# Hybrid gMLP/SSD block: dt moved into the exponent of the decays, x copied by ScalarE, products inside the chunk issued two steps at a time, ScalarE's decays listed by pairs

## The chip, the cores and the metric

The kernel runs on one core of a Trainium2 chip. The metric is the device time of one execution in microseconds (us), the median of three runs. A profile records one further execution: its rows give start and duration of the instructions of TensorE (PE, with its weight loads as PEld), VectorE (DVE), ScalarE (ACT), GpSimd (POOL) and of the DMA queues.

## What is computed

One layer of a decoder trunk over 1024 positions of width 1024 in float32: an input projection, a chunked gMLP branch, a Mamba-2 (SSD) branch, their gated merge and an output projection. The change touches the SSD branch alone. It has 32 heads of 64 channels in 8 groups of 4 heads, and walks the sequence in 8 chunks of 128 positions:

```python
xd = x * dt[..., None]
a_cs = cumsum(dt * a)                      # inside a chunk
cb = einsum('clgn,csgn->cgls', cc, bc)     # C_l . B_s
y_diag = einsum('cgls,cgrls,csgrp->clgrp', cb, exp(a_cs[l] - a_cs[s]) for s <= l, xd)
chunk_states = einsum('csgn,cgrs,csgrp->cgrpn', bc, exp(a_cs[-1] - a_cs[s]), xd)
state = state * exp(a_cs[-1]) + chunk_states      # over the chunks
y_off = einsum('clgn,cgrpn,cgrl->clgrp', cc, prev_states, exp(a_cs))
y = y_diag + y_off + x * d_skip
```

## The kernel before

**Stages.** Up to about 905 us of the span the kernel forms the input projections. Then comes the SSD stage, and behind it the projection of the SSD branch, the merge and the output. In the SSD stage TensorE alternates between the SSD work and the projection of the gMLP branch (`proj_a`), which is drawn from a generator: one `draw` issues two matmuls of 512 columns into the two banks `pma`. There are 192 draws; they fill TensorE's list between pieces of SSD work.

**Steps.** The SSD work is cut into 32 steps, `order[n] = (g, s)`: group g and a pair s of chunks. The order takes two groups side by side, (0,0), (1,0), (0,1), (1,1), ..., so s runs from 0 to 3 within eight steps, and steps 2k and 2k+1 are the same pair of chunks of two groups. A step consists of:

- `fetch`: loads `dcy`, the cumulative sums of 4 heads by 256 positions broadcast to 128 partitions, and `sl`, the slices of B, C, x and z. Five sets of buffers go round.
- `mask` (lines L1155 and L1159): two ACT instructions write `ea` = exp(a_cs) from `dcy`; then one POOL select overwrites the upper triangle of `dcy` with -1e30, in place, so it can't begin before both have read it.
- `decay` (L1167): eight ACT instructions turn `dcy` into exp(dcy - a_cs[s]), in place, so they can't begin before the select is done.
- `prep`: TensorE forms C.B in bank `pc`, and transposes B into `pc` and x into bank `px`; DVE multiplies `dcy` by C.B (L1183), and forms x·dt (`xd`) and x·dt·exp(..) (`xe`) from `px` (both L1186); ACT copies the transposed B into `bn` (L1190). Accesses to one bank keep their order in the program, so `bn` waits for L1183.
- `front`: sixteen matmuls of 64 columns `yi` <- `xd`, `dcy` (the product inside the chunk), then what strips are due (`pq`, matmuls of 32 columns that sum squares for a later norm), then `sp` <- `bn`, `xe` (the chunk states); DVE adds `sp` to the state (`add_state`, L1236), forms `y` from `yi` (L1216), and POOL scales the state for the next addition (`mul_state`, L1228).
- `back`: TensorE multiplies the states by C into `yn`; DVE forms `ym` = `yn`·`ea` (L1262); POOL adds it to `y` (L1264) and multiplies by the gate into `yz` (L1265). For every odd s the squares of `yz` (ACT, L1289) and their sum (POOL, L1293) follow some steps later, and once a group a root on POOL (L1320).

**What sets the order.** TensorE's instructions stand in program order. `link(key, f)` ties each instruction of ACT (`"A"`), DVE (`"V"`) and POOL (`"G"`) in these steps behind the one linked before it on that engine: the order in which the code names them is the order in which the engine's list holds them. An instruction that waits therefore holds up all linked ones behind it.

The loop of step n goes: `front(n)`; then `ahead_of(n)`, which lists the decays of step n+2, the first `mul_state` of step n+1, a sum or a root if one is due, and the mask of step n+3; then 4 or 5 draws; `back(n)`; `prep(n+2)`; `fetch`. So between the select of one step and that of the next POOL's list holds one whole step of other work.

**Banks.** Of PSUM's eight banks six rotate under the tag `bk` and two under `px`; `bank()` sends every fourth request to `px`.

Of the kernel before, what the change touches and what calls it, by code (L numbers as in the profile page):

```python
# [8 lines left out]
F32 = mybir.dt.float32  # L9
# [26 lines left out]
def hybrid_kernel(  # L36
# [493 lines left out]
    def bank(name):  # L530

        if pairs_done:
            pairs_done.append(name)
            if len(pairs_done) % 4 == 2:
                return psum.tile([P, 512], F32, name=name, tag="px", bufs=2)
        return psum.tile([P, 512], F32, name=name, tag="bk", bufs=6)

# [3 lines left out]
    def later(delay, f, *a):  # L541
        tasks.append((slot[0] + delay, f, a))
# [172 lines left out]
    def dt_part2(dth, adt):  # L715
        n = NCH * NH
        pa = bank("pacs")
        mm(pa[:, 0:n], tri, adt)
        mm(pa[:, n : 2 * n], ones, adt)
        V.tensor_scalar_mul(nacs, pa[:, 0:n], -1.0)  # L720
        A.activation(cd, pa[:, n : 2 * n], AF.Exp)
        V.tensor_add(dde, pa[:, n : 2 * n], nacs)
        A.activation(dde, dde, AF.Exp)
        V.tensor_mul(dde, dde, dthq)
        later(3, dt_part3)

    def dt_part3():
# [401 lines left out]
    class Group:  # L1129


        def __init__(self, g):
            self.g, self.pre, self.st, self.yz, self.y = g, {}, None, {}, {}

        def fetch(self, s):
            g, nm = self.g, f"{self.g}_{s}"
# [24 lines left out]

        def decay(self, s):

            dcy, sub = self.pre[s][1], fac(nacs, self.g, s)
            for i in range(2):
                for h in range(HPG):
                    link("A", lambda: A.activation(dcy[:, h, i, :], dcy[:, h, i, :], AF.Exp,  # L1167
                                                   bias=sub[:, i, h : h + 1]))

        def prep(self, s):  # L1170
            g, nm = self.g, f"{self.g}_{s}"
            sl, dcy, ea = self.pre[s]
            px, pc = bank(f"px{nm}"), bank(f"pc{nm}")
            for i in range(2):
                tsl = slice(i * P, (i + 1) * P)
                mm(pc[:, i * P : (i + 1) * P], sl[:, 1, tsl], sl[:, 0, tsl])
                tp(pc[:, 256 + i * P : 256 + (i + 1) * P], sl[:, 1, tsl], ident)
                tp(px[:, i * 256 : i * 256 + P], sl[:, 2, tsl], ident)
                tp(px[:, i * 256 + P : i * 256 + 256], sl[:, 3, tsl], ident)
            x4 = px.rearrange("p (i h w) -> p i h w", i=2, h=HPG)  # L1180
            xs = []
            d3 = dcy.rearrange("p h i l -> p h (i l)")
            link("V", lambda: V.tensor_tensor(d3, d3, pc[:, 0:256].unsqueeze(1).to_broadcast([P, HPG, 256]), op=ALU.mult))  # L1183
            for v, f in (("xd", dthq), ("xe", dde)):
                t = p2x.tile([P, 512], F32, name=f"{v}{nm}", tag=v, bufs=3)
                link("V", lambda: V.tensor_tensor(t.rearrange("p (i h w) -> p i h w", i=2, h=HPG), x4,  # L1186
                                    fac(f, g, s).unsqueeze(3).to_broadcast([P, 2, HPG, HD]), op=ALU.mult))
                xs.append(t)
            bn = p2x.tile([P, 256], F32, name=f"bn{nm}", tag="bn", bufs=3)
            link("A", lambda: A.copy(bn, pc[:, 256:512]))  # L1190
            self.pre[s] = (sl, dcy, bn, xs[0], xs[1], ea)

        def front(self, s):

            g, nm = self.g, f"{self.g}_{s}"
            sl, dcy, bn, xd, xe, ea = self.pre[s]
            yi = bank(f"yi{nm}")
# [356 lines left out]
    def draw(n):  # L1554
        for _ in range(n):
            left[0] -= next(fill, 1) is None
# [6 lines left out]
    def ahead_of(n):  # L1563

        with tc.high_priority():
            decays(n + 3)
            if n + 1 < len(order) and order[n + 1][1]:
                groups[order[n + 1][0]].mul_state(order[n + 1][1], 0)
            for _ in range(1 if n < 29 else 2):
                beside_step()  # L1570
            masks(n + 4)

    def step(n, *fs):
        for f in fs:
            item(getattr(groups[order[n][0]], f), order[n][1])

    draw(6)
    for n in range(2):
        step(n, "front")
        ahead_of(n)  # L1580
        draw(10)
    for n in range(len(order)):
        if n > 1:
            step(n, "front")
            ahead_of(n)
            draw(6 if n == 2 else 4 + n % 2)
# [5 lines left out]
        fetch(n + 6)  # L1592
    while tasks or work or posts:
        draw(2)
        run_tasks()
        beside_step()
        while posts:
            p, q, sq = posts.pop(0)
            p.post2(q, sq)


    room.extend(ea_r[0] + [st_tag])
# [470 lines left out]
```

## Time and profile before

| | |
|---|---|
| median of three runs | 1361.64 us (1361.04 to 1362.76) |
| profiled execution, its own time | 1362.27 us |
| its span, first to last instruction | 1360.4 us |
| granted TensorE clock, mean | 0.998 |
| first and last product inside the chunk (`yi`) | at 910.8 and 1106.8 us |

The span is what the trace covers; the 1.9 us beside it lie outside the first and the last instruction. Rows of the timeline give start, duration, engine, line and tiles; `x8` is the number of instructions merged into a row; what stands in brackets is the idle time before and what ended it. A matmul's recorded duration is longer than its share of TensorE, because matmuls overlap in the pipeline: what a matmul costs is read from the distance of two starts. In a row that groups instructions the number behind `|` is their busy time and then the mean duration of one in ns, and behind the second `|` stands the idle time in front of them with what ended it.

### The profile page before, as it was taken

The page shows a single profiled execution, that of the slowest core. Times are in us where ns is not written, and L with a number is a line of the kernel's source. Part 1 is how long each engine was busy: PE and PEld are TensorE (multiplying, and loading weights), DVE is VectorE, ACT ScalarE, POOL GpSimd, SP SyncE. Part 2 cuts the span into 40 slices and gives each one's busy share as a digit, 9 for nine tenths or more (in the row PEclk, how much of TensorE's full clock was granted, in tenths as well). Part 3 has the DMA queues.
Part 4 walks back from the last instruction along what each step waited for, and adds up shares of the span by engine and source line. Part 5 has one row for each costly group of instructions (what it writes and reads, how often), then busy time and mean ns, then how long its engine had stood idle before and what let it go on. Part 6 is the DMA issues. An engine that isn't in the chain of part 4 may idle for free.

```text
span 1360.4 us, 20108 instructions
## 1 busy us (share of the span) xinstructions
PE 1347.0 (99%) x6907; PEld 1114.4 (82%) x6907; DVE 1056.1 (78%) x1731; ACT 800.4 (59%) x1446; POOL 196.1 (14%) x193
## 2 busy tenths in 40 slices
PE   8999999999999999999999999999999999999997
PEld 6688888888888888888888888888888888888886
DVE  4776786787777898688887788358888877959976
ACT  5754666666657665466576655486877834233453
POOL 1000000000000000000000000007798981000002
PEclk9999999999999999999999999999999999999999
DMA  9675444333345667777656866489889878888913
GB/s 292 177 248 142 134 124 124 117 119 122 101 132 155 193 184 231 248 216 246 202 192 193 244 204 186 154 289 318 302 297 311 306 256 291 313 261 317 381 45 124
DMA packets 249577, 288.64 MB, mean 212 GB/s; under 512 B 16860, under 2 KB 196484, under 8 KB 249476
## 3 DMA queue, kind: packets, MB, share of 16 engines
q1 hardware_dynamic: 174868, 203.80, 47.0%
q10 hardware_dynamic: 74544, 83.57, 18.0%
q8 instruction: 54, 0.88, 0.3%
q14 instruction: 47, 0.39, 0.1%
q0 software_dynamic: 64, 0.00, 0.0%
HBM read 199.82 MB, written 87.49 MB: 211 GB/s over the span
## 4 chain that ended last, share of the span: by engine, by line
PE 93%; POOL 3%; DMA 1%; issue 1%; ACT 1%; DVE 1%; SPq 0%; POOLq 0%; DVEq 0%; ACTq 0%
PE xcb L585 6%; PE xz L585 6%; PE xuz L585 6%; PE xx L585 6%; PE xg L585 6%; PE pma L82 5%; PE ox L1914 3%; PE yuz L585 3%; PE yx L585 3%; PE ycb L585 3%; PE yp L1722 3%; PE yz L585 3%; PE vx L990 3%; PE yg L585 3%; PE oy L1914 2%; PE x0p L1722 2%
## 5 line engine op out<-in xcount | busy, mean ns | idle before, releaser
L1159 POOL TENSOR_SCALAR_AFFINE_SELECT dcy<-dcy 128x1024 f32<-128x1024 f32 x32 | 35.3, 1103 | 788.7 <-ACT ea L1155 788.7
L1167 ACT ACTIVATE dcy<-dcy,nacs 128x128 f32<-128x128 f32 x256 | 78.3, 389 | 2.9 <-POOL dcy L1159 2.4
L1183 DVE TENSOR_TENSOR dcy<-dcy,pc 128x1024 f32<-128x1024 f32 x32 | 39.0, 1218 | 8.0 <-PE pc L85 5.8
L1265 POOL TENSOR_TENSOR yz<-y,sl 128x512 f32<-128x512 f32 x32 | 44.7, 1396 | 2.5
L82 PE MATMUL pma<-yh,wah 128*128 128x512 f32 x128 | 43.2, 418 | 0.0
L82 PE MATMUL pma<-yh,wal 128*128 128x512 f32 x128 | 42.6, 413 | 0.0
L82 PE MATMUL pma<-yl,wah 128*128 128x512 f32 x128 | 40.2, 395 | 0.0
L1155 ACT ACTIVATE ea<-dcy 64x512 f32<-64x512 f32 x64 | 39.8, 622 | 0.4
L1190 ACT COPY bn<-pc 128x256 f32<-128x256 f32 x32 | 11.9, 371 | 46.4 <-DVE dcy L1183 44.9
L1060 ACT ACTIVATE ac<-ac 128x1024 f32<-128x1024 f32 x32 | 33.9, 1060 | 8.1 <-DVE ac L1058 7.9
L1264 POOL TENSOR_TENSOR y<-y,ym 128x512 f32<-128x512 f32 (+1 forms) x32 | 37.4, 1170 | 1.8 <-DVE ym L1262 1.8
L1058 DVE SCALAR_TENSOR_TENSOR ac<-c2x,cwt,ac 128x1023 f32<-128x1023 f32 (+2 forms) x24 | 30.7, 1278 | 8.8 <-ACT ac L1056 8.7
L1058 DVE SCALAR_TENSOR_TENSOR ac<-c2cb,cwt,ac 128x1023 f32<-128x1023 f32 (+2 forms) x24 | 30.7, 1278 | 8.2 <-ACT ac L1056 8.0
L1929 POOL TENSOR_TENSOR r<-r,fnw 128x512 f32<-128x512 f32 x4 | 6.1, 1534 | 207.3 <-ACT junk L1927 207.3
L82 PE MATMUL yi<-dcy,xd 128*64 128x128 f32 x512 | 35.0, 279 | 0.0
L1262 DVE TENSOR_TENSOR ym<-yn,ea 128x512 f32<-128x512 f32 (+1 forms) x32 | 19.9, 621 | 18.2 <-PE yn L82 18.0
L1653 DVE SCALAR_TENSOR_TENSOR yn<-yn,par,rb 128x512 f32<-128x512 f32 x32 | 26.1, 822 | 9.1 <-DMA yn<-yb_d 9.1
L82 PE MATMUL sp<-xe,bn 128*128 128x256 f32 x112 | 32.7, 409 | 0.0
L82 PEld LDWEIGHTS yn<-sl,st 128*128 128x128 f32 x224 | 29.8, 191 | 2.8 <-POOL st L1228 0.4
L82 PEld LDWEIGHTS yi<-dcy,xd 128*64 128x64 f32 x512 | 27.3, 136 | 5.7 <-issue 3.2
L1058 DVE SCALAR_TENSOR_TENSOR ac<-c1cb,cwt,ac 128x1023 f32<-128x1023 f32 (+2 forms) x24 | 30.6, 1276 | 1.3 <-ACT ac L1056 1.3
L1022 ACT ACTIVATE vm<-vm,vr 128x128 f32<-128x128 f32 x64 | 25.5, 483 | 10.1 <-DMA vm<-v_d 9.6
(2983 smaller groups left out, 4368.4 us busy)
## 6 DMA issues: line engine op xcount, KB each, us to landing
sl<-s_d SPq DMA_DIRECT2D x32, 768.0 KB
s_d<-ac ACTq DMA_DIRECT2D x32, 512.0 KB
wb_d<-wbb ACTq DMA_DIRECT2D x32, 512.0 KB
dcy<-acs_d SPq DMA_DIRECT2D x32, 512.0 KB
av<-in_w_in_dram SPq DMA_DIRECT2D x36, 256.0 KB
aw<-in_ada_w_dram SPq DMA_DIRECT2D x16, 512.0 KB
wbr<-in_w_proj_b_dram SPq DMA_DIRECT2D x32, 256.0 KB
yb_d<-yz ACTq DMA_DIRECT2D x32, 256.0 KB
```

Source lines behind the costliest of these rows:

```text
L82: pin(PE.matmul(acc, l, r, start=first, stop=last))
L585: pin(PE.matmul(ps, lw[:, k * P : (k + 1) * P], r[k], start=first and n + k == 0, stop=n == 2 and k == 3, skip_group_check=not first))
L990: pin(PE.matmul(ps[pn][j], l[:, j * P : (j + 1) * P], r, start=nm in ("p1", "p5", "p2") and n + units[i][1] == 0, stop=n == 2 and k == 3, ...
L1058: V.scalar_tensor_tensor(ac[:, s:], cc[:, : S - s], conv_wt[:, 3 - s, i : i + 1], ac[:, s:], op0=ALU.mult, op1=ALU.add)
L1155: link("A", lambda: A.activation(ea[hh * HD : (hh + 1) * HD], dcy.rearrange("p (j e) i l -> p e j (i l)", e=2)[hh * HD : (hh + 1) * HD, hh ...
L1159: link("G", lambda: G.affine_select(out=d8, in_=d8, compare_op=ALU.is_ge, fill=-1e30, base=0, pattern=[[0, 2 * HPG], [1, P]], channel_mult ...
L1167: link("A", lambda: A.activation(dcy[:, h, i, :], dcy[:, h, i, :], AF.Exp, bias=sub[:, i, h : h + 1]))
L1183: link("V", lambda: V.tensor_tensor(d3, d3, pc[:, 0:256].unsqueeze(1).to_broadcast([P, HPG, 256]), op=ALU.mult))
L1264: link("G", lambda: G.tensor_add(y1[:, :, t0:], y1[:, :, t0:], m[:, :, t0:]))
L1265: link("G", lambda: G.tensor_mul(yz, y1, sl[:, 4:6]))
L1722: pin(PE.matmul(ps[j], a[:, v, js], r, start=first and n + k == 0, stop=n == 2 and k == KT - 1, skip_group_check=not first))
L1914: pin(PE.matmul(ps, a[:, tsl], b[:, cs], start=first and n + j == 0, stop=n == 2 and j == 3, skip_group_check=not first))
```

## The change

- `dthq`, so far dt, is turned into ln(dt) minus the cumulative sum once `dde` has been formed from it: a maximum and an addition on DVE and a logarithm on ACT, each on 128x256. `decay` takes it as its bias in place of `nacs`, so that `dcy` holds the decay times dt.
- `prep` no longer forms x·dt on DVE: ACT copies the transposed x out of `px` (tile `xd`), ahead of the DVE instruction that reads the same bank for `xe`.
- The 16 `yi` matmuls move from `front` to a new `inner`. From step 2 on `inner` runs for steps n and n+1 together in front of `front(n)`, n even, with the strips behind them. The draws of two steps stay nine in sum: three stand ahead of the two `inner`, two behind `front(n)`, four behind `front(n+1)`.
- From step 2 on the masks and decays are no longer listed in `ahead_of` but at the end of the new `behind(n)`, after `back(n)`, `prep(n+2)` and `fetch`: for n even the decays of step n+3; for n odd the mask of n+3, the decays of n+3 and then the mask of n+4.
- `px` and `pc` get the two banks `px` for themselves; all else shares the six others.

```diff
         if pairs_done:
             pairs_done.append(name)
-            if len(pairs_done) % 4 == 2:
+            if name[:2] in ("px", "pc"):
                 return psum.tile([P, 512], F32, name=name, tag="px", bufs=2)
...
         V.tensor_mul(dde, dde, dthq)
+        V.tensor_scalar_max(dthq, dthq, 1e-37)
+        A.activation(dthq, dthq, AF.Ln)
+        V.tensor_add(dthq, dthq, nacs)
...
-            dcy, sub = self.pre[s][1], fac(nacs, self.g, s)
+            dcy, sub = self.pre[s][1], fac(dthq, self.g, s)
...
-            xs = []
+            xr = p2x.tile([P, 512], F32, name=f"xd{nm}", tag="xd", bufs=3)
+            link("A", lambda: A.copy(xr, px))
             d3 = dcy.rearrange("p h i l -> p h (i l)")
             link("V", lambda: V.tensor_tensor(d3, d3, pc[:, 0:256].unsqueeze(1).to_broadcast([P, HPG, 256]), op=ALU.mult))
-            for v, f in (("xd", dthq), ("xe", dde)):
...
+            xe = p2x.tile([P, 512], F32, name=f"xe{nm}", tag="xe", bufs=3)
+            link("V", lambda: V.tensor_tensor(xe.rearrange("p (i h w) -> p i h w", i=2, h=HPG), x4,
+                                fac(dde, g, s).unsqueeze(3).to_broadcast([P, 2, HPG, HD]), op=ALU.mult))
...
-        def front(self, s):
...
+        def inner(self, s):
+
+            dcy, xd = self.pre[s][1], self.pre[s][3]
+            self.yi[s] = yi = bank(f"yi{self.g}_{s}")
             for i in range(2):
                 for h in range(HPG):
                     j, hh = h // 2, h % 2
                     mm(yi[hh * HD : (hh + 1) * HD, j * 256 + i * P : j * 256 + (i + 1) * P],
                        xd[:, i * 256 + h * HD : i * 256 + (h + 1) * HD], dcy[:, h, i, :])
-            while posts:
-                p, q, sq = posts.pop(0)
-                p.post2(q, sq)
+
+        def front(self, s):
...
-            decays(n + 3)
+            if n < 2:
+                decays(n + 3)
             if n + 1 < len(order) and order[n + 1][1]:
                 groups[order[n + 1][0]].mul_state(order[n + 1][1], 0)
             for _ in range(1 if n < 29 else 2):
                 beside_step()
-            masks(n + 4)
+            if n < 2:
+                masks(n + 4)
...
+    def inners(*ns):
+        with tc.high_priority():
+            for n in ns:
+                groups[order[n][0]].inner(order[n][1])
+            strips()
+
+    def behind(n):
         step(n, "back")
         if n == 1:
             draw(4)
         if n + 2 < len(order):
             step(n + 2, "prep")
         fetch(n + 6)
+        with tc.high_priority():
+            if n % 2 == 0:
+                decays(n + 4)
+            else:
+                masks(n + 4)
+                decays(n + 4)
+                masks(n + 5)
...
+    for n in range(2, len(order)):
+        if n % 2 == 0:
+            draw(3)
+            inners(n, n + 1)
+        step(n, "front")
+        ahead_of(n)
+        draw(4 if n % 2 else 3 if n == 2 else 2)
+        behind(n)
```

(`masks(m)` and `decays(m)` bring the steps up to m-1 into the list that are not in it yet.)

More of the change, by code (lines that the diff above doesn't have):

```diff
@@ L1132, in __init__ @@
         def __init__(self, g):
-            self.g, self.pre, self.st, self.yz, self.y = g, {}, None, {}, {}
+            self.g, self.pre, self.st, self.yz, self.y, self.yi = g, {}, None, {}, {}, {}
         def fetch(self, s):
@@ L1202, in front @@
                        xd[:, i * 256 + h * HD : i * 256 + (h + 1) * HD], dcy[:, h, i, :])
-            while posts:
-                p, q, sq = posts.pop(0)
-                p.post2(q, sq)
+        def front(self, s):
+            g, nm = self.g, f"{self.g}_{s}"
+            sl, _, bn, _, xe, _ = self.pre[s]
+            yi = self.yi.pop(s)
             sp = bank(f"sp{nm}")
@@ L1575, in step, with strips @@
             item(getattr(groups[order[n][0]], f), order[n][1])
[L1577 to L1586, printed above, removed]
+    def strips():
+        while posts:
+            p, q, sq = posts.pop(0)
+            p.post2(q, sq)
+    def inners(*ns):
[4 more added lines that the diff above has]
+    def behind(n):
         step(n, "back")
@@ L1592, in hybrid_kernel @@
         fetch(n + 6)
+        with tc.high_priority():
[5 more added lines that the diff above has]
+                masks(n + 5)
+    draw(6)
+    for n in range(2):
+        inners(n)
+        step(n, "front")
+        ahead_of(n)
+        draw(10)
+    for n in range(2):
+        behind(n)
[3 more added lines that the diff above has]
+            inners(n, n + 1)
+        step(n, "front")
+        ahead_of(n)
+        draw(4 if n % 2 else 3 if n == 2 else 2)
+        behind(n)
     while tasks or work or posts:
@@ L1596, in hybrid_kernel @@
         beside_step()
-        while posts:
-            p, q, sq = posts.pop(0)
-            p.post2(q, sq)
+        strips()
     room.extend(ea_r[0] + [st_tag])
```

9 lines of the change are left out of this document (1 added, 8 removed).

## The prediction

> **What bounds the kernel now.** First the page: its totals, its slices and the granted clock.
>
> ```profile
> span 1360.4 us, 20108 instructions
> PE 1347.0 (99%) x6907; PEld 1114.4 (82%) x6907; DVE 1056.1 (78%) x1731; ACT 800.4 (59%) x1446; POOL 196.1 (14%) x193
> ...
> POOL 1000000000000000000000000007798981000002
> PEclk9999999999999999999999999999999999999999
> ```
>
> TensorE is busy throughout, so a microsecond taken from or added to its list is one of the whole. But POOL's 196.1 us lie almost all in nine slices: the stage that the change rewrites. So next I read that stage alone: from the products of step 4 to those of step 28 (24 steps), first TensorE's timeline for the two ends, then POOL's sum over that window (length, busy time, instructions), then its groups there.
>
> ```profile
> 942.53 0.66 PE L82 MATMUL yi<-dcy,xd 128*64 128x128 f32 x8
> ...
> 1088.94 0.55 PE L82 MATMUL yi<-dcy,xd 128*64 128x128 f32 x6
> ```
>
> ```profile
> 942.53:1088.94 146.41, 127.97 (x124) 1.00 0.90 306
> ```
>
> ```profile
> L1265 POOL TENSOR_TENSOR yz<-y,sl 128x512 f32<-128x512 f32 x24 | 33.4, 1390 | 1.9
> L1159 POOL TENSOR_SCALAR_AFFINE_SELECT dcy<-dcy 128x1024 f32<-128x1024 f32 x24 | 26.6, 1107 | 15.7 <-ACT ea L1155 15.6
> L1228 POOL TENSOR_TENSOR st<-st,cd 128x256 f32<-128x256 f32 x36 | 21.5, 613 | 0.9 <-DVE st L1234 0.8
> ```
>
> Two steps take 146.41 / 12 = 12.20 us. POOL works 127.97 / 12 = 10.66 us of them, and of its 18.4 idle microseconds 15.6 are waits of the select for ACT's `ea`. POOL is thus 1.5 us per pair of steps away from being the bound. The chain of waits, asked for 1038 to 1042 us, shows that it is that at places already:
>
> ```profile
> 1038.65 1.18 POOL st L1228 x2
> 1039.82 1.25 POOL yz L1293
> 1041.07 0.04 issue
> 1041.12 0.42 PE pq L82 x8
> ```
>
> The strip `pq` starts as soon as POOL's sum is done: there TensorE waits for POOL. DVE's groups in the same window say the same of the state, on which `yn` depends; their first row is for later:
>
> ```profile
> L1183 DVE TENSOR_TENSOR dcy<-dcy,pc 128x1024 f32<-128x1024 f32 x25 | 30.5, 1219 | 6.8 <-PE pc L85 4.9 <-ACT ea L1155 0.7 <-ACT dcy L1167 0.5
> ...
> L1186 DVE TENSOR_TENSOR xd<-px,dthq 128x512 f32<-128x512 f32 x24 | 16.4, 682 | 0.0
> ...
> L1236 DVE TENSOR_TENSOR st<-st,sp 128x256 f32<-128x256 f32 x36 | 14.9, 414 | 5.0 <-POOL st L1228 4.7 <-issue 0.2
> ```
>
> **The change, part by part.**
>
> *Products of two steps together.* TensorE's timeline of step 7:
>
> ```profile
> 959.90 0.27 PE L85 MATMUL pc<-ident,sl 128*128 128x128 f32 x1
> 960.01 0.38 PE L85 MATMUL px<-ident,sl 128*128 128x128 f32 x2
> 960.33 1.09 PE L82 MATMUL yi<-dcy,xd 128*64 128x128 f32 x16
> 961.35 0.42 PE L82 MATMUL pq<-yz,ones 128*32 128x128 f32 x8
> ```
>
> ```profile
> 960.33 0.98 PE L82 MATMUL yi<-dcy,xd 128*64 128x128 f32 x14
> ```
>
> Matmuls of full width follow each other by 0.11 us (959.90 to 960.01), so `yi` could start at 960.23; it starts at 960.33, 0.10 later. The second fence, a narrower window of the same view, counts 14 of the 16: two matmuls of 64 columns cost 1.09 - 0.98 = 0.11 together, eight such pairs 0.88; the group takes 1.02 to the next one. Entering and leaving the narrow shape thus costs 0.10 + 0.14 = 0.24 us; what the first wide matmul behind it loses I bound by 0 and another 0.11. I take 0.30. There were 32 groups; after there are 17 (steps 0 and 1 alone, 15 pairs): 15 x 0.30 = **-4.5 us** (-3.6 to -5.3).
>
> *x copied by ACT, dt in the exponent.* In the window DVE loses 24 instructions `xd` (row above) and ACT gains as many copies. ACT's sum over the window, its group `bn` there, and from its groups over the whole span the nearest row for such a copy, 128x512 out of a bank, and the table load beside the dt work:
>
> ```profile
> 942.53:1088.94 146.41, 112.49 (x297) 1.00 0.90 306
> ```
>
> ```profile
> L1190 ACT COPY bn<-pc 128x256 f32<-128x256 f32 x24 | 8.9, 372 | 31.8 <-DVE dcy L1183 30.3 <-DMA wa<-in_w_proj_a_dram 1.4
> ```
>
> ```profile
> L601 ACT COPY c1x<-xx 128x512 f32<-128x512 f32 x16 | 9.3, 582 | 1.6 <-PE xx L585 1.1 <-PE yx L585 0.5
> ```
>
> ```profile
> L721 ACT ACT_TABLE_LOAD  x1: 1283/1283/1283, 722.5 to 722.5; - x1
> ```
>
> ACT is busy 112.49 of 146.41 and idles 31.8 in front of `bn`, whose bank DVE still reads. The copy needs only `px`, so its 24 x 0.58 = 14 us fit in that idle time: 0. If the cover were gone, ACT would need (112.5 + 14) / 12 = 10.5 us per pair plus its waits, still under 12.2. The logarithm costs ACT a table load of 1.28 us or two, once, at a time when TensorE has draws of its own: 0, at most 3.
>
> *ACT's list by pairs.* This is where the time goes. ACT's, then POOL's timeline around the selects of two steps:
>
> ```profile
> 957.35 2.44 ACT L1167 ACTIVATE dcy<-dcy,nacs 128x128 f32<-128x128 f32 x8
> 959.70 1.26 ACT L1155 ACTIVATE ea<-dcy 64x512 f32<-64x512 f32 x2
> 962.15 0.99 ACT L1167 ACTIVATE dcy<-dcy,nacs 128x128 f32<-128x128 f32 x3
> ```
>
> ```profile
> 961.02 1.09 POOL L1159 TENSOR_SCALAR_AFFINE_SELECT dcy<-dcy 128x1024 f32<-128x1024 f32 x1 [0.27 <-ACT ea L1155]
> 962.08 1.29 POOL L1264 TENSOR_TENSOR y<-y,ym 128x512 f32<-128x512 f32 x1
> 963.45 1.29 POOL L1265 TENSOR_TENSOR yz<-y,sl 128x512 f32<-128x512 f32 x1
> 964.70 1.28 POOL L1293 TENSOR_TENSOR yz<-yz 128x512 f32<-128x512 f32 x1
> 965.92 1.10 POOL L1159 TENSOR_SCALAR_AFFINE_SELECT dcy<-dcy 128x1024 f32<-128x1024 f32 x1
> ```
>
> A select ends at 962.11, and the decays that wait for it start at 962.15: 0.04. Eight decays take 2.35 to the first `ea` (957.35 to 959.70); from there the two `ea` and the start of the select take 1.32 (to 961.02). So from the end of one select to the start of the next there are at least 0.04 + 2.35 + 1.32 = **3.71 us** when ACT runs decays and `ea` between. Before, POOL spends them on a whole step of other work (the rows at 962.08, 963.45, 964.70), and the second select starts without a wait. After, behind every odd n from 3 to 27 the list says mask n+3, decays n+3, mask n+4: the two selects are neighbours on POOL, and the second waits 3.71 us for the ACT work that the first one released. Behind it queue both `mul_state`, the additions and products of the next two steps, the sums and the roots; for them wait `add_state` on DVE and so `yn` on TensorE, and the strips.
>
> In the Trainium skill, "TensorE: Matmul & The Clock Gate", the section on the architecture of the array says that ScalarE, VectorE and GpSimd work their queues strictly in order and that TensorE alone pulls work forward. By that rule nothing fills the gap, and the sum is the one below; if POOL could pass a waiting select, only the first part's -4.5 us would be left. The rows above agree with it: each select, waiting or not, stands where the list has it.
>
> **Sum.** From one double select to the next POOL then needs 10.66 + 3.71 = 14.37 us, against TensorE's 12.20 - 0.30 = 11.90. Twelve such intervals: 12 x (14.37 - 11.90) = +29.6. With -4.5 of the fewer groups: +25.1. A lead of POOL at the beginning I take as 0: in the first interval the select starts some 3 us behind `prep` (DVE's 1.22 for `dcy`, `bn`, `ea`), the second 3.71 + 1.1 later, and the `mul_state` for step n+2, two instructions behind, comes out within a microsecond of the time `yn` needs it. So 1362.27 + 25.1 = 1387.4 for the profiled execution; the median stood 0.6 lower: **1387 us**.
>
> Bounds: a lead of one whole gap (-3.7), gaps of 3.5, and `yz` at the 1.29 of the timeline where its mean is 1.39 (-2.4) give 1378. ACT's other work slipped into the gaps (a cast of 0.62, a store that waits for `yz`), 0.6 to 1.2 in each of 12, gives 1394 to 1402.
>
> **Rivals.**
>
> 1. *TensorE stays the bound* (faster). It decides as soon as POOL's own work between two double selects is under 11.90 - 3.71 = 8.2 us, or if other POOL work gets between the two selects. Then only the groups count: 1361.6 - 4.5 = **1357**. For it: POOL's spans are modelled roughly. Against it: 10.66 us, of which the select, `yz`, `y` and `mul_state` recur in each step, and the ties between linked instructions leave nothing that could go between. 0.11. A shade of it, in which the groups' gain and a short-lived queue cancel: 1361, 0.03.
> 2. *Half a queue*: POOL's lead and the pairs with little POOL work (s = 0: no state to scale, halves of `y`) leave TensorE the bound in half of the intervals: +14.8 - 4.5, **1372**. For it: sums and roots come in bunches. Against: the mean counts, as long as POOL never catches up within an interval. 0.08.
> 3. *The queue and more*. `yi` of two steps, `pq`, `sp` and the two `pma` fill all six banks of `bk`, where `px` and `pc` shared eight with them; where a block of `pma` ends, the next two banks wait for two DVE evictions of about 0.7 us (row of `xd`, same shape): 7 x 1.4 = 10, together **1397**. Before, the profile has no such wait. 0.10.
> 4. *The clock drops.* TensorE would stand about 2.5 us in each interval. The slices above show full clock, with no such stand in the stage, so the trace can't tell what that does; were half the clock granted for as long as the stand again, 12 x 1.2 = +15: **1402**. The Trainium skill, "TensorE: Matmul & The Clock Gate", Part 1, puts the idle window after which the clock halves at about 3.4 us; by that rule 2.5 us stay below, and only a wait run together would trip it. 0.04.
>
> The forecast keeps 0.64.
>
> **How the numbers follow.** A measurement can tell about 0.2% (2.7 us) from no change here. Faster by more: rival 1, 0.11. Within: 0.03. Slower: 0.64 + 0.08 + 0.10 + 0.04 = 0.86. The range reaches from between rival 2 and its nearest bound, 1366, to the upper bound, 1402; it leaves out rival 1 and its shade and a part of rival 4.
>
> **What would show it.** The idle time of L1159 for `ea` rises from 15.6 us to some 45 us (12 x 3.7), in waits of 3 to 4 us, one per pair. From step 4 to step 28 the stage takes some 172 us in place of 146.4. Idle time appears on TensorE in front of `yn` (or of the strips), with DVE's state addition behind POOL as releaser; before there is next to none. `yi` is entered 17 times, and between the 16 matmuls of one step and those of the next there is no loss of 0.24 us. The `xd` rows of DVE are gone, ACT has 32 copies of about 0.6 us, and ACT's idle time before `bn` shrinks. The forecast is wrong if the neighbouring selects show no wait, if POOL works its list with the gap and `yn` still doesn't wait, or if TensorE waits at `yi` for ACT's copy or for a bank instead.

## The result and the profile after

The changed kernel takes 1425.21 us (median of four runs, 1423.46 to 1427.35), the kernel before 1362.10 beside it (1361.04 to 1362.76): 1.046 times as long, 95% interval 1.045 to 1.0475, or +63 us. The forecast was +25. The profiled execution took 1427.35 us. From its page the totals, POOL's slices and the granted clock:

```profile
span 1425.6 us, 20108 instructions
...
PE 1363.4 (96%) x6907; PEld 1126.8 (79%) x6907; DVE 1039.0 (73%) x1701; ACT 820.3 (58%) x1480; POOL 195.3 (14%) x193
...
POOL 1000000000000000000000000265666682000002
PEclk9999999999999999999999999999989999999999
```

POOL does the same work as before (195.3 us against 196.1) in slices that were 7 to 9 tenths full and now mostly are 5 to 6. The same stretch as in the prediction, from the products of step 4 to those of step 28, first with TensorE's busy time, then with POOL's (window, length, busy time and instructions, granted clock, share of the DMA engines, GB/s):

```profile
944.65:1149.63 204.98, 162.41 (x1173) 0.89 0.64 220
```

```profile
944.65:1149.63 204.98, 127.42 (x125) 0.89 0.64 220
```

The stretch is 204.98 - 146.41 = 58.6 us longer, of 65.2 by which the span grew; the rest lies in the steps on either side of it. POOL's busy time is the 127.97 of before less half a microsecond. So POOL is not busier: it stands for 77.6 us. Where it stands, and who else waits, is in the groups of that stretch, POOL's, DVE's, TensorE's and ACT's:

```profile
L1162 POOL TENSOR_SCALAR_AFFINE_SELECT dcy<-dcy 128x1024 f32<-128x1024 f32 x24 | 26.3, 1095 | 60.0 <-ACT ea L1158 59.9
...
L1232 POOL TENSOR_TENSOR st<-st,cd 128x256 f32<-128x256 f32 x36 | 22.4, 640 | 0.0
```

```profile
L1240 DVE TENSOR_TENSOR st<-st,sp 128x256 f32<-128x256 f32 x36 | 15.1, 419 | 58.8 <-POOL st L1232 41.7 <-issue 7.5 <-POOL dcy L1162 6.0
```

```profile
L82 PE MATMUL yn<-sl,st 128*128 128x128 f32 x168 | 30.6, 322 | 41.3 <-DVE st L1238 19.6 <-DVE st L1240 19.4 <-DVE y L1220 2.3
...
L82 PE MATMUL yi<-dcy,xd 128*64 128x128 f32 x384 | 23.7, 276 | 0.0
```

```profile
L1185 ACT COPY xd<-px 128x512 f32<-128x512 f32 x24 | 14.1, 587 | 9.6 <-PE px L85 9.3
```

The select waits 60.0 us for `ea` (15.7 before), then the state addition for POOL's `mul_state` (41.7, where it was 4.7), then `yn` for DVE's work on the state (39.0). That is the chain the prediction named, at the place it named. `yi` waits for nothing: neither for ACT's copy, which costs 0.587 us as estimated, nor for a bank.

**One pair of steps.** POOL's timeline, from the first select of one pair to the first of the next:

```profile
979.09 1.09 POOL L1162 TENSOR_SCALAR_AFFINE_SELECT dcy<-dcy 128x1024 f32<-128x1024 f32 x1
985.32 1.09 POOL L1162 TENSOR_SCALAR_AFFINE_SELECT dcy<-dcy 128x1024 f32<-128x1024 f32 x1 [5.14 <-ACT ea L1158]
986.38 0.61 POOL L1232 TENSOR_TENSOR st<-st,cd 128x256 f32<-128x256 f32 x1
...
996.83 1.10 POOL L1162 TENSOR_SCALAR_AFFINE_SELECT dcy<-dcy 128x1024 f32<-128x1024 f32 x1 [3.08 <-ACT ea L1158]
```

The second select waits 5.14 us, and the first of the next pair again 3.08. That second wait isn't in the forecast. It isn't the rule either: of the twelve first selects of the stretch four wait (1.96, 3.08, 1.98 and 2.16 us, together 9.2), and eight follow POOL's own work without a pause, as the one at 979.09 does. The pair shown is also one of the three at s = 0, whose long waits at `yn` (L1238, the copy that starts a state) make 19.6 of the 39.0 us. What lies between the selects on the other engines, DVE first:

```profile
987.03 0.42 DVE L1240 TENSOR_TENSOR st<-st,sp 128x256 f32<-128x256 f32 x1 [7.27 <-POOL st L1232]
987.37 0.42 DVE L1266 TENSOR_TENSOR ym<-yn,ea 128x256 f32<-128x256 f32 x1
987.70 1.21 DVE L1187 TENSOR_TENSOR dcy<-dcy,pc 128x1024 f32<-128x1024 f32 x1
988.83 0.68 DVE L1189 TENSOR_TENSOR xe<-px,dde 128x512 f32<-128x512 f32 x1
989.43 0.41 DVE L1238 COPY st<-sp 128x256 f32<-128x256 f32 x1
...
992.93 1.22 DVE L1187 TENSOR_TENSOR dcy<-dcy,pc 128x1024 f32<-128x1024 f32 x1 [1.34 <-PE pc L85]
```

TensorE:

```profile
989.90 1.23 PE L82 MATMUL yn<-sl,st 128*128 128x128 f32 x4 [6.22 <-DVE st L1238]
990.92 0.63 PE L82 MATMUL pc<-sl 128*128 128x128 f32 x2
```

And ACT (ACTq are its DMA issues):

```profile
979.17 2.43 ACTq L94 DMA_DIRECT2D yb_d<-yz  x2
981.65 2.45 ACT L1170 ACTIVATE dcy<-dcy,dthq 128x128 f32<-128x128 f32 x8 [5.66 <-DMA sl<-s_d]
984.00 1.25 ACT L1158 ACTIVATE ea<-dcy 64x512 f32<-64x512 f32 x2
...
990.40 2.43 ACT L1170 ACTIVATE dcy<-dcy,dthq 128x128 f32<-128x128 f32 x8
...
994.18 0.37 ACT L1192 COPY bn<-pc 128x256 f32<-128x256 f32 x1 [0.30 <-DVE dcy L1187]
...
995.50 1.26 ACT L1158 ACTIVATE ea<-dcy 64x512 f32<-64x512 f32 x2
```

Read in order of time it is a ring, in this pair. Second select (985.32), `mul_state` (986.38), state addition (987.03). Behind it in DVE's list stand `ym`, the product into `dcy`, `xe` and then the state copy of the other step (989.43), for which `yn` waits on TensorE (989.90). Behind `yn` stands the `prep` of that step, whose `pc` DVE needs for the next product into `dcy` (992.93); ACT's decays (990.40), which that product needs too, end at the same time, at 992.83. Then `bn` (994.18), squares, `ea` (995.50) on ACT, and the next first select (996.83). That select starts the gap of the next pair. From first select to first select it is 996.83 - 979.09 = 17.74 us, in the mean 204.98 / 12 = 17.1. No engine is full in it; each waits for another.

The gap here is 1.43 longer than the 3.71 of the forecast: the first select ended at 980.18, but ACT's decays started at 981.65, behind two stores of `yz` that it issued from 979.17 to 981.60. (The row names a load in place of them; the times fit the stores.) Eight of the twelve second selects wait 3.71 or 3.72 us, four wait 4.23 to 5.90.

### The profile page after: what moved, and what is told of

Its sections match the earlier page's. It is cut to its first block, busy times and chain, and to the rows that moved or that the text cites. A ratio compares the mean times of both kernels' runs of the same rounds, so it can differ in the third digit from the quotient of the medians.

```text
span 1425.6 us, 20108 instructions
## 1 busy us (share of the span) xinstructions
PE 1363.4 (96%) x6907; PEld 1126.8 (79%) x6907; DVE 1039.0 (73%) x1701; ACT 820.3 (58%) x1480; POOL 195.3 (14%) x193
## 4 chain that ended last, share of the span: by engine, by line
PE 81%; POOL 5%; issue 5%; DMA 4%; ACT 2%; DVE 1%; SPq 1%; ACTq 0%; POOLq 0%; DVEq 0%
PE xcb L585 6%; PE xz L585 6%; PE xuz L585 6%; PE xx L585 6%; PE xg L585 5%; PE ox L1944 3%; PE yuz L585 3%; PE yx L585 3%; PE ycb L585 3%; PE vx L993 3%; PE yp L1752 3%; PE yz L585 3%; PE yg L585 3%; PE oy L1944 2%; PE pma L82 2%
## 5 line engine op out<-in xcount | busy, mean ns | idle before, releaser
L1170 ACT ACTIVATE dcy<-dcy,dthq 128x128 f32<-128x128 f32 x256 | 78.3, 389 | 34.9 <-POOL dcy L1162 14.2
L82 PE MATMUL yn<-sl,st 128*128 128x128 f32 x224 | 38.8, 312 | 43.6 <-DVE st L1240 21.0
L82 PEld LDWEIGHTS yn<-sl,st 128*128 128x128 f32 x224 | 33.8, 214 | 51.4 <-DVE st L1240 25.0
L1240 DVE TENSOR_TENSOR st<-st,sp 128x256 f32<-128x256 f32 x48 | 20.1, 418 | 67.1 <-POOL st L1232 47.2
L82 PE MATMUL pma<-yl,wah 128*128 128x512 f32 x128 | 46.8, 449 | 0.0
L1269 POOL TENSOR_TENSOR yz<-y,sl 128x512 f32<-128x512 f32 x32 | 41.8, 1306 | 10.7 <-issue 8.4
L82 PE MATMUL yi<-dcy,xd 128*64 128x128 f32 x512 | 32.0, 276 | 0.1
```

What stands on the lines that cost most here:

```text
L82: pin(PE.matmul(acc, l, r, start=first, stop=last))
L1269: link("G", lambda: G.tensor_mul(yz, y1, sl[:, 4:6]))
```

## The experiments

Times are medians, with lowest and highest, and the ratio to the kernel before on the same chip with its 95% interval. In each set the kernel before took 1361.9, 1361.6, 1362.3 and 1362.4 us.

### Is it the list? The changed kernel with the list by steps

```diff
-            if n < 2:
-                decays(n + 3)
+            decays(n + 3)
...
-            if n < 2:
-                masks(n + 4)
+            masks(n + 4)
...
-            if n % 2 == 0:
-                decays(n + 4)
-            else:
-                masks(n + 4)
-                decays(n + 4)
-                masks(n + 5)
```

> The changed kernel with the lists of masks and decays put back to where they stood before (one mask a step, ahead of the draws); pairs of products, copy, dt and banks stay. List theory (the two neighbouring selects on POOL with ACT's decays between them make the whole loss): 1355 to 1360 us, some 4.5 us under the kernel before, and no wait of the select over 1 us in the mean. Rival, ACT's copies and logarithm are too much for it: 1370 us or more, with TensorE waiting at yi. Rival, the six banks: 1367 or more, with TensorE waiting at pma or yn for an eviction.

1367.95 us (1365.59 to 1369.41), 1.0038 [1.0023, 1.0052]. The list is 57 of the 63 us. But the 4.5 us of the fewer groups don't appear: the kernel stays 6 above before (3 to 7 by the interval). TensorE's stretch of the same steps, and its and ACT's timeline at a place where it loses:

```profile
944.20:1093.50 149.30, 144.20 (x1175) 1.00 0.89 301
```

```profile
1030.25 1.09 PE L82 MATMUL yi<-dcy,xd 128*64 128x128 f32 x16
1032.02 1.09 PE L82 MATMUL yi<-dcy,xd 128*64 128x128 f32 x16 [0.68 <-DMA tha<-th_d]
```

```profile
1030.06 1.25 ACT L1158 ACTIVATE ea<-dcy 64x512 f32<-64x512 f32 x2
1031.34 0.59 ACT L1185 COPY xd<-px 128x512 f32<-128x512 f32 x1
```

TensorE works 144.20 us of 149.30 and stands for 5.1; before it worked 146.26 of 146.41. Two groups should follow each other after some 1 us; here they are 1.77 apart, because ACT copies the second x only at 1031.34, behind decays and `ea` (it ends at 1031.93, `yi` starts at 1032.02). The row names a DMA, but the copy's end is what fits: a releaser is inferred, and the neighbouring engine's timeline decides.

### Is it that the two selects are neighbours on POOL? ACT's list kept, the second select listed later

```diff
-                masks(n + 5)
+                masks(n + 5, True)
...
     def behind(n):
         step(n, "back")
+        with tc.high_priority():
+            selects()
```

The mask called with `True` lists `ea` alone; `selects()` lists the select, now behind the next step's `y` and `yz`.

> The changed kernel with ACT's list untouched; only POOL's second select of a pair is listed later, behind the additions and products (y, yz) of the next step. List theory in its narrow form (what hurts is that POOL stands idle and holds up what is behind): 1356 to 1370 us. Rival, ACT's own order (mask, decays, mask, with the wait for POOL inside) is the loss: 1390 us or more.

1391.71 us (1389.68 to 1394.23), 1.0215 [1.0199, 1.0231]. 33 us go, 30 stay: the range of the rival, ACT's own order. The waits of the SSD stage, 905 to 1140 us (sum in us, times, longest), and TensorE's stretch:

```profile
ACT dcy L1174 <- POOL dcy L1166: 24.1, 19, 3.0
DVE dcy L1191 <- ACT dcy L1174: 21.2, 20, 1.8
```

```profile
943.90:1114.80 170.90, 149.75 (x1173) 0.98 0.75 262
```

Now ACT waits for the select, and DVE for ACT. Opening POOL's list alone moves the wait to the next engine of the ring: 170.90 / 12 = 14.2 us a pair.

### Is the list enough by itself? The kernel before with the list by pairs

```diff
-            decays(n + 3)
+            if n < 2:
+                decays(n + 3)
...
-            masks(n + 4)
+            if n < 2:
+                masks(n + 4)
...
+            if n % 2 == 0:
+                decays(n + 4)
+            else:
+                masks(n + 4)
+                decays(n + 4)
+                masks(n + 5)
```

> The kernel before with nothing of the change but the lists by pairs (decays; mask, decays, mask at the end of each step). List theory: 1412 to 1435 us, as much as the whole change. Rivals (copies, banks, pairs of products): 1362 to 1375 us.

1442.69 us (1442.01 to 1445.69), 1.0592 [1.0577, 1.0608]: the list alone costs 81, more than in the whole change and more than expected. Its waits in the stretch:

```profile
DVE st L1236 <- POOL st L1228: 45.0, 9, 5.8
...
PE pq L82 <- POOL yz L1293: 39.8, 8, 5.8
```

With the products of one step at a time the strips come directly behind `yi`, and TensorE meets POOL's late sums there. Why the same list costs less in the change was not tried; there the strips come once per pair, behind both products.

### Copy, dt and banks without the pairs of products

```diff
-        if n % 2 == 0:
-            draw(3)
-            inners(n, n + 1)
+        inners(n)
...
-        draw(4 if n % 2 else 3 if n == 2 else 2)
+        draw(6 if n == 2 else 4 + n % 2)
```

This stands on the first experiment's kernel.

> As the first run of this call (lists as before), but the products of each step stand alone again in front of its chunk states: what is left of the change is ACT's copy, dt in the exponent and the banks. List theory with groups worth 0.30 us each: 1361 to 1363 us, so 4 to 5 us above the first run. If the groups are worth nothing: as the first run.

1363.41 us (1362.99 to 1364.53), 1.0005 [0.9995, 1.0015]. The copy by ACT, dt in the exponent, its logarithm and the new banks cost nothing that can be told. The forecast that this kernel lies above the first experiment's missed: it lies 4.5 below. So pairs of products, meant to give 4.5, cost that much even where the list is in order.

### The pairs of products alone

The kernel before with `inner` in pairs and the new banks; DVE forms `xd`, the bias is `nacs`, the list goes by steps.

```diff
-            link("A", lambda: A.copy(xr, px))
...
+            link("V", lambda: V.tensor_tensor(xr.rearrange("p (i h w) -> p i h w", i=2, h=HPG), x4,
+                                fac(dthq, g, s).unsqueeze(3).to_broadcast([P, 2, HPG, HD]), op=ALU.mult))
```

> The kernel before with the pairs of products and the banks of the change alone: DVE forms x times dt, the bias is the cumulative sum, masks and decays are listed by steps. Groups at 0.30 us each and nothing late: 1356 to 1359 us. If DVE's x times dt comes too late for the second product (it ends some 2.0 to 2.6 us behind prep, where the product starts 2.4 behind it): 1360 to 1370 us.

1373.53 us (1372.40 to 1375.28), 1.0082 [1.0066, 1.0097]: 12 above before, beyond what either theory gave. Against the first experiment (6 above) it shows what the copy by ACT is worth where products come in pairs: about 6 us. That it does so by taking work from DVE is argued, not shown.

### More cover ahead of the pair

The first experiment's kernel with five draws ahead of the two `inner` and two behind each front.

```diff
-            draw(3)
+            draw(5)
             inners(n, n + 1)
...
-        draw(4 if n % 2 else 3 if n == 2 else 2)
+        draw(3 if n == 2 else 2)
```

> As the first experiment (masks and decays listed by steps, all else of the change), but five of the nine draws of a pair stand ahead of the two products, and two behind each front. Late-copy theory (the first experiment loses its gain because the second product of a pair waits for ACT's copy of x, issued only about 2.4 us before): 0.9 us more of time there, 1357 to 1361 us, no wait at the second yi. If the pairs cost for another reason: 1366 to 1369 as before, or more where yn now waits for DVE.

1370.79 us (1370.51 to 1371.30), 1.0062 [1.0048, 1.0076]: the theory of the late copy missed. The wait at the second `yi` is gone, but cover put ahead of `yi` is missing ahead of `yn`, where TensorE now stands for 4.3 us (2.7 in the first experiment).

### Is the ring cut at `bn`?

```diff
-            link("A", lambda: A.copy(bn, pc[:, 256:512]))
+            link("V", lambda: V.tensor_copy(bn, pc[:, 256:512]))
```

> The changed kernel with one edit: DVE instead of ACT copies the transposed B (bn) out of the bank pc. POOL's and ACT's lists of masks and decays stay, the two selects stay neighbours. Loop theory (the wait for the second select goes on through DVE's state addition, DVE's product into dcy and ACT's copy bn to the next mask, so that a pair takes the length of this loop, 17.1 us, and not POOL's work plus one gap, 14.4): the loop is cut at bn, a pair comes near 14.4 to 15.5, 1390 to 1408 us. Throughput theory of the prediction plus other causes (clock, DMA): 1420 to 1430 us, no change.

1420.26 us (1419.55 to 1422.09), 1.0429 [1.0409, 1.0449]: only 5 us. The loop theory missed; the time lies in the range given for no change. POOL's timeline of the same pair of steps:

```profile
978.15 1.28 POOL L1269 TENSOR_TENSOR yz<-y,sl 128x512 f32<-128x512 f32 x1
979.38 1.09 POOL L1162 TENSOR_SCALAR_AFFINE_SELECT dcy<-dcy 128x1024 f32<-128x1024 f32 x1
984.18 1.09 POOL L1162 TENSOR_SCALAR_AFFINE_SELECT dcy<-dcy 128x1024 f32<-128x1024 f32 x1 [3.71 <-ACT ea L1158]
```

Here, as in the changed kernel, the first select follows POOL's own `yz` without a pause, and the second waits its 3.71. The first selects of the stretch together wait 4.4 us in place of 9.2, and the 4.8 between them is about what the run gains. So the way through `bn` is worth some 5 us; for the rest POOL's additions and products, which hang on `ym`, come before the first select. That these too hang all the way round on the second select of the pair before is argued from the time, not traced link by link.

### Is it the clock?

The changed kernel with 8 or 16 further matmuls (their results are overwritten) ahead of `yn` in every odd step from step 3 on, where TensorE stands.

```diff
             yn = bank(f"yn{self.g}_{s}")
+            if self.g % 2 and order.index((self.g, s)) > 1:
+                for _ in range(8 if s else 16):
+                    mm(yn[:, P : 2 * P], sl[:, 0, P : 2 * P], sl[:, 0, P : 2 * P])
```

> The changed kernel with extra matmuls (8, or 16 at s = 0, of 128 columns, 1.8 or 3.5 us at full clock) into the bank yn ahead of the products of the states in the odd step, where TensorE waits; their results are overwritten. Clock theory (of the 58.6 us that steps 4 to 28 take more, some 16 to 20 come from the half clock granted after the waits): clock back near 1.0, 1405 to 1418 us in spite of the added work. If the clock costs nothing: 1425 us or, where the added matmuls stick out, up to 1435.

1429.99 us (1429.39 to 1432.71), 1.0500 [1.0481, 1.0518]: 4.8 above the changed kernel, in the range given for a clock that costs nothing. TensorE's stretch:

```profile
947.10:1150.10 203.00, 179.60 (x1415) 0.97 0.63 219
```

The granted clock rises from 0.89 to 0.97 and the stretch shrinks by 2.0 us only. The run doesn't separate the clock's share: what the higher clock gives, the added matmuls can take in front of `yn`. It shows that the stretch holds 242 more recorded matmul instructions, 17 us of busy time, and doesn't grow. It also shows something that wasn't asked. The added matmuls read only `sl`, no state, and yet TensorE stands for 18.8 us in front of them until DVE's state addition (L1240) is done. That addition also reads `sp`, so the likely reason is that `yn` gets the bank that `sp` held; which bank it was wasn't traced. So a part of the wait at `yn` is perhaps one for a bank.

### Where does POOL's gap enter the ring? `mul_state` on DVE

```diff
-                link("G", lambda: G.tensor_mul(v3(self.next), v3(self.st),
+                link("V", lambda: V.tensor_mul(v3(self.next), v3(self.st),
```

In the changed kernel:

> The changed kernel with one edit: the scaling of the state (mul_state) runs on DVE, not on POOL; masks, decays and the neighbouring selects stay. Loop theory (select, decays, mask, select on ACT and POOL; then the state's scaling on POOL; then state addition, ym, the product into dcy on DVE; then yn and prep on TensorE; then ACT again): the loop is cut where it leaves POOL for DVE, and what is left is ACT's own order: 1380 to 1400 us, and no wait of TensorE at yn over 2 us. If the loss were POOL's work plus the gaps alone (the prediction's sum, now 1.8 us a pair less work): 12.6 us a pair, 1362 to 1370. If neither: 1415 or more.

1398.08 us (1397.69 to 1399.94), 1.0267 [1.0253, 1.0281]: 27 us go, as the ring's theory had it (1380 to 1400), where the sum of POOL's work and one gap would have 1362 to 1370. The theory's second sign, no wait at `yn` over 2 us, missed: the longest is 4.5, and all together are 23.2 us, where they were 41.3. The waits of the same steps:

```profile
POOL dcy L1162 <- ACT ea L1158: 57.7, 16, 6.2
...
PE yn L82 <- DVE st L1240: 11.4, 8, 2.7
```

The selects wait nearly as long as in the changed kernel, 57.7 us, but less of the wait reaches `yn` (11.4, where this releaser had 19.4). Had POOL's work plus one gap set the pace, 22 us less on POOL would have brought the time down to about that of before. But the run doesn't tell a link that is cut from a round that is shorter by POOL's work: POOL's busy time falls from 127.42 to 106.81 us, the stretch from 204.98 to 177.50.

On the experiment with copy, dt and banks alone:

> As the fourth experiment (lists by steps, products of each step alone), with the scaling of the state on DVE. TensorE is the bound there: 1361 to 1364 us, no gain, so that the difference from the run two above is what the pairs are worth once POOL is relieved (4 to 5 us).

1363.65 us (1362.68 to 1365.13), 1.0012 [1.0003, 1.0021]. Taking 22 us off POOL gives nothing where the list goes by steps, so POOL's work didn't bound the kernel before. The comparison with the pairs came out the other way than expected: with pairs the same kernel takes 9 us more (1372.49, next section), not 4 to 5 less.

### Do the pairs of products gain with POOL relieved?

The first experiment's kernel with `mul_state` on DVE:

> As the first experiment (masks and decays by steps, all else of the change), with the scaling of the state on DVE. If POOL's closeness to the bound eats the gain of the pairs: 1356 to 1360 us, under the kernel before. If ACT's copy coming late is what eats it: 1362 to 1367.

1372.49 us (1371.34 to 1372.93), 1.0076 [1.0062, 1.0089]: above both ranges, 5 slower than with `mul_state` on POOL. And with one draw moved ahead of the pair and the strips in the other two banks:

```diff
-            if name[:2] in ("px", "pc"):
+            if name[:2] in ("px", "pc", "pq"):
...
-            draw(3)
+            draw(4)
             inners(n, n + 1)
...
-        draw(4 if n % 2 else 3 if n == 2 else 2)
+        draw(3 if n % 2 or n == 2 else 2)
```

> As the run before it in this call, with four of the nine draws ahead of a pair of products (then two, then three), and the strips in the two banks of px. 0.5 us more for ACT's copy and no wait of the chunk states for a strip's eviction: 1354 to 1358 us; same as the run before if neither mattered.

1373.49 us (1373.26 to 1374.17), 1.0084 [1.0071, 1.0098]: no gain, so neither mattered. With products in pairs no arrangement tried reaches the time before, and the waits that remain are short and scattered over `yn`, `yi` and `sp`.

### Both masks ahead of the decays

If the loss comes from the decays that stand between the two selects, exchanging two entries of the list has to take it away.

```diff
-                masks(n + 4)
-                decays(n + 4)
                 masks(n + 5)
+                decays(n + 4)
```

(One `masks(n + 5)` lists both masks.)

> The changed kernel with two list entries of the odd steps in another order: both masks first, then the decays (mask n+3, mask n+4, decays n+3). The selects stay neighbours on POOL and ACT's entries stay by pairs, but no decays lie between the two selects, so the second waits only for two more ea (1.26 us, while the first select runs): the gap of 3.71 us falls to under 0.3. List theory: most of the loss goes, 1362 to 1378 us, TensorE's waits at yn under 8 us in steps 4 to 28. If what hurts is that both masks of a pair stand in one step at all (POOL's and ACT's bunched work): 1385 us or more. A later load of the second step's dcy could show as a wait of ea for a DMA.

1378.31 us (1375.71 to 1379.50), 1.0116 [1.0098, 1.0134]: 0.3 above the range of the list theory, with waits at `yn` of 8.2 us in these steps, where 8 were the limit named and 41.3 stood before the exchange. POOL's timeline of the same pair, and TensorE's stretch:

```profile
984.33 1.09 POOL L1162 TENSOR_SCALAR_AFFINE_SELECT dcy<-dcy 128x1024 f32<-128x1024 f32 x1 [3.01 <-ACT ea L1158]
985.62 1.09 POOL L1162 TENSOR_SCALAR_AFFINE_SELECT dcy<-dcy 128x1024 f32<-128x1024 f32 x1 [0.20 <-ACT ea L1158]
```

```profile
945.20:1101.90 156.70, 145.55 (x1175) 1.00 0.81 284
```

The second select still follows the first directly, but its `ea` no longer stands behind the first one's decays: it waits 0.20 us in place of 5.14, and 47 of the 63 us are gone. With `mul_state` on DVE as well:

> As the run before it in this call, with the scaling of the state on DVE as well. If what is left of that run's waits at yn comes from POOL (state behind two selects): 1358 to 1366 us, under it by 5 or more. If it comes from ACT's list (copy, decays) or DVE's: within 3 us of it or slower, as it was for the lists by steps.

1380.13 us (1378.26 to 1381.04), 1.0129 [1.0113, 1.0145]: nothing more. So POOL's state work is not shown to be in the remaining 16 us, though with the list by steps the same move cost 4.5 us by itself (1372.49 against 1367.95) and could hide as much. The cause isn't settled beyond the 6 that pairs of products cost with the list by steps.

No version beats the kernel before; the change without its pairs (1363.41) equals it.

## Why the prediction was right and wrong

**What bounds the kernel before.** That a microsecond of TensorE is one of the whole held for waits: the stretch grew by what TensorE stands, 204.98 - 162.41 = 42.6 us, plus 16 us that its own work took longer (162.41 against 146.26), at a lower clock. That POOL is close to being the bound was true as a sum and meant nothing yet: relieving it by 22 us changed nothing (1363.65 against 1363.41).

**Products of two steps together.** The size was right. From TensorE's timeline after, step 4 with step 5:

```profile
944.65 1.97 PE L82 MATMUL yi<-dcy,xd 128*64 128x128 f32 x32
946.55 1.13 PE L82 MATMUL sp<-xe,bn 128*128 128x256 f32 x4
947.33 0.81 PE L82 MATMUL pma<-yl,wah 128*128 128x512 f32 x2
...
950.43 1.03 PE L82 MATMUL sp<-xe,bn 128*128 128x256 f32 x4
951.11 0.58 PE L82 MATMUL pma<-yh,wah 128*128 128x512 f32 x1
```

Two steps' products take 1.90 us to the next instruction, where two single groups took 2 x 1.02: 0.14. One entry of 0.10 falls away. And `sp` right behind them takes 0.78 (946.55 to 947.33), 0.68 elsewhere (950.43 to 951.11): another 0.10, the loss of the first wide matmul that was bounded by 0 and 0.11. Together 0.34 per group saved, against the 0.30 taken. What failed is the step from there to the time: the gain counted as -4.5 while the pair's demand counted as nothing. A pair needs the second step's x, decays and product into `dcy` a step earlier; with the list by steps the pairs cost more than they save (1367.95 against 1363.41 without pairs). That the early need is the whole reason isn't shown: of the 5.1 us that TensorE stands there, 1.6 are at `yi`, 2.7 at `yn` and 0.8 at `sp`.

**Copy by ACT, dt in the exponent.** Right: 0 forecast, 1.0005 [0.9995, 1.0015] measured.

**List by pairs.** Mechanism, place and gap right: the second select waits for what the first released, 3.71 us forecast, and 3.71 or 3.72 in eight of twelve pairs, as here in POOL's timeline some steps earlier:

```profile
969.33 1.09 POOL L1162 TENSOR_SCALAR_AFFINE_SELECT dcy<-dcy 128x1024 f32<-128x1024 f32 x1 [3.72 <-ACT ea L1158]
```

The list alone makes the loss: without it +6, alone +81.

**Sum.** This is the step that failed. It took the interval of POOL as its work plus one gap, 10.66 + 3.71 = 14.37 us, so it had POOL working without pause from the second select to the next first one, and put every other wait of POOL at nothing without a reason. The runs show 17.1: POOL's work is as forecast (127.42 / 12 = 10.62), but it idles 77.6 / 12 = 6.5 a pair, not 3.7. About 33 us beyond twelve gaps of 3.71 remain, in four places: 9.2 in front of first selects, 6.2 in the four second selects that waited longer than 3.71, 10.1 in front of `yz` and 8.1 in front of `y`, most of these behind DVE's `ym`. (Of the 10.1 two waits, 4.0 and 4.4, have no releaser in the trace; both end within 0.2 us of the strips' matmuls, which read a `yz`.)

So TensorE, DVE and ACT stand while POOL waits, and POOL then waits for what they do late. In the pair shown the rows give one such way round: a first select whose `ea` hangs on the second select of the pair before, by `mul_state`, DVE, then `yn` and `prep` or the decays, and ACT. A throughput sum holds as long as the work ahead of the gap doesn't depend on the work behind the last one. In that pair it does; that the whole 17.1 is the length of such rings is argued. For it: 22 us of work taken off POOL bring 27 back, where the sum would have brought some 55 to 63. The exchange of two list entries bears on the gap, not on this: it takes the gap itself away and gives 47 with no work changed on any engine, and the sum without a gap would have TensorE as the bound as well. The upper bound had slipped ACT work in the gaps at 0.6 to 1.2 each; in the pair shown it was 1.43, from stores, but over the twelve pairs only 6.2 / 12 = 0.5, so this doesn't carry the time out of the range.

**The rivals.** That TensorE stays the bound, or that half the queue shows, is refuted by the 60.0 us in front of the selects. The banks cost nothing at `yi`, which idles 0.0, and nothing without the list by pairs (1363.41); at `yn` the added matmuls leave a wait for a bank open. The dropping clock came true: waits at `yn` reach 7.6 us where 2.5 were forecast, and some waits under 3 us were followed by half the clock too (last section). TensorE's busy time is 18 us above that of the first experiment (162.41 against 144.20) for the same matmuls. How much of it is in the total isn't separated; in the pair shown a faster TensorE would have gained next to nothing, since ACT's decays ended when `pc` did.

**Strict order of the lists.** The rule of the Trainium skill that the prediction cites ("TensorE: Matmul & The Clock Gate", on strict queues) held: nothing passed the waiting select (no row of POOL starts between 979.09 and 985.32), and 47 us hung on the order of entries.

## What to carry to other kernels

When an edit puts a wait on an engine, ask whether what the engine waits for depends, through the other engines' lists, on what this engine did behind its last wait; if so, add the links of one round and compare that length with the busiest engine's sum. A sum of work and one wait is then only a lower bound: here 14.4 us a pair, against 17.1. Two instructions of one engine that each need a partner's work in between are listed so that the partner finishes its preparation for both first, or with other work between them. Work grouped to save switches on one engine is due earlier on all the others, and that is priced before the saving is counted.

## What the runs showed of the hardware

**Half clock after a wait.** TensorE's windows around the wait for the state at 983.70:

```profile
983.70:989.90 6.20, 0.00 (x0) 0.84 0.46 183
989.90:993.90 4.00, 4.00 (x16) 0.50 0.72 233
```

For 6.2 us no matmul ran; over the next 4.0 the granted clock was 0.50, and matmuls of full width, 0.11 us apart at full clock, followed at 0.21 (two in the 0.42 from 990.92 to 991.34). The mean over the stretch fell to 0.89. Two shorter waits of the same run, each 1.95 us long, with what follows them:

```profile
957.60:959.00 1.40, 1.40 (x6) 0.50 0.04 12
1006.92:1008.00 1.08, 1.08 (x9) 1.00 0.00 0
```

After the one that ended at 957.59 the granted clock was 0.50, after the one that ended at 1006.92 it was 1.00; after a wait of 2.92 us (to 1022.52) it was 0.50 again. The Trainium skill, "TensorE: Matmul & The Clock Gate", Part 1, gives an idle window of about 3.4 us after which the clock halves. The wait of 6.2 us agrees with it; those of 1.95 and 2.92 show that here the clock can halve after less, so the length of one wait doesn't decide it.

**Stores in front of compute.** Two stores issued from ACT's list took 2.43 us (979.17 to 981.60) and held up the decays behind them by 1.43. What the second store waited for isn't settled, and moving the stores to another queue wasn't tried.
